# Two gated feed-forwards by seven block products for eight, with modulation loads moved to an earlier stage

## The chip, the cores and the metric

The kernel runs on one core of a Trainium2 chip. TensorE (PE) multiplies, VectorE (DVE), ScalarE (ACT) and GpSimd (POOL) do elementwise work, and SyncE (SP) issues most transfers. The metric is the device time of one execution in microseconds (us), lower is better, as the median of several runs.

## The reference, cut to what matters

A residual stream h of 512 tokens x 1024 features, batch 1, goes through two blocks, all in float32. The first block has sliding-window attention, a feed-forward with a causal convolution, a gated delta net, and the second such feed-forward. The second block, to which the change belongs, is modulated: nine vectors of 1024 numbers come from the condition c.

```python
def modulate(h, shift, scale):
    return h * (1 + scale[:, None, :]) + shift[:, None, :]

def swiglu(h, w_in, w_down):
    g, u = jnp.split(h @ w_in, 2, axis=-1)      # w_in 1024 x 5632
    return (jax.nn.silu(g) * u) @ w_down        # w_down 2816 x 1024
...
mod = jax.nn.silu(c) @ w_ada[l] + b_ada[l]
sh1, sc1, gt1, sh2, sc2, gt2, sh3, sc3, gt3 = jnp.split(mod, N_ADA, axis=-1)

h = modulate(rmsnorm(x, g_ffn1[l]), sh1, sc1)
x = x + 0.5 * gt1[:, None, :] * swiglu(h, w_ffn1_in[l], w_ffn1_down[l])
...
x = x + gt2[:, None, :] * (y @ w_out[l])

h = modulate(rmsnorm(x, g_ffn2[l]), sh3, sc3)
x = x + 0.5 * gt3[:, None, :] * swiglu(h, w_ffn2_in[l], w_ffn2_down[l])
```

## The kernel before, in words

**Layout.** Features lie on the 128 partitions and tokens along the free dimension, so h is eight tiles of 128 x 512. Each product of matrices in float32 is three passes of TensorE in the fp32r type: a weight tile w is split into a rounded high part wh and the rest wl, the moving operand x into xh and xl, and `mm3` adds wh·xh, wh·xl and wl·xh into one PSUM tile of 128 x 512.

**Weights.** The host packs all weights into blocks of 512 KB in the order in which the program takes them: 8 tiles of 128 x 128, 128 x 1024 numbers. `wtile` loads a block into a raw tile `wr` on SP's queue, ScalarE casts it to `wh` (CAST), VectorE subtracts for `wl`. In the delta-net stage alone (`by_dma`), `wl` is made in another way: ScalarE writes -wh and a transfer that GpSimd issues adds the raw block to it from memory. The raw, high and low tiles share twelve wide buffers of 128 x 1024 (pool "b"), with at most 3 raw, 4 high, and 4 low at a time (WRAW, WPART).

**Stages.** They run in the order swa, ffn0, gdn, ffn1, glu1, mix, glu2, final. ffn0 and ffn1 are the convolution feed-forwards of the first block, glu1 and glu2 the gated ones of the second. In `glu_ffn`, m runs over 22 pairs of tiles, gate m and up 22 + m. A tile is `gemm`: 8 k, 24 matmuls on 512 columns. ScalarE takes silu of the gate, VectorE multiplies by up, and `split` gives xh and xl for the down projection. That runs in two parts, after m = 10 and after m = 21 (`to_residual`): eight output tiles of 11 k each, added to h with the gate vector. The last two output tiles of a stage are computed in halves of 256 tokens, and the next stage's norm (`norm_halves`) and first three tiles (`gemm_halves`) too, so that a stage's first matmuls stand beside the norm of the second half.

**Modulation.** 72 blocks of w_ada (`ada`) are loaded into `wa` and reduced by one VectorE instruction each, against silu(c). 24 are done in ffn0, one for each m; 48 in glu1, three for each m below 16.

**Order.** A recorder collects all operations in program order. A planner gives each a cost and a priority, which is the program order plus a bias, and writes one static order for each engine; line L406, in the recorder, issues them all, so rows are told apart by tile names. PSUM has eight banks with caps by use (BANKS: three for `mm`). `nc.after` gives operations a further predecessor.

Of the kernel before, what the change touches and what calls it, by code (L numbers as in the profile page):

```python
# [19 lines left out]
KD = D // 128  # L20
# [474 lines left out]
class Kernel:  # L495
# [48 lines left out]
    def ps(self, shape=(128, S), tag="ps", bufs=None):  # L544
        return self.nc.pool_tile(self.pp, list(shape), F32, "ps", self.nm(tag), 8, BANKS[tag])

# [754 lines left out]
    def norm_modulated(self, n):  # L1301
# [9 lines left out]
                nc.vector.scalar_tensor_tensor(l, u, shift[:, k:k + 1], h.bitcast(F32), ALU.add, ALU.subtract)  # L1311
        return xs

    def gated(self, gate):
        def add(m, ps, t):
            self.nc.vector.scalar_tensor_tensor(self.h[m][:, t], ps, gate[:, m:m + 1], self.h[m][:, t],
                                                ALU.mult, ALU.add)
        return add
# [11 lines left out]
            nc.scalar.copy(t[r0 + 32:r0 + 64], sin[r0 + 32:r0 + 64])  # L1330
            self.tab.append(t)

    def glu_ffn(self, i, fill=lambda m: None):
        nc = self.nc
        xs = self.norm_modulated(f"ffn{i}")
        hs = []
        head = self.gemm_halves([(f"glu{i}", 0), (f"glu{i}", 22), (f"glu{i}", 1)], xs)
        tile = lambda m: head.pop(0) if head else self.gemm(f"glu{i}", m, xs)
        for m in range(22):
            if i == 1 and m == 16:  # L1340
                nc.after = (len(nc.ops) - 1,)
                self.tables()
                nc.after = ()
            g = self.act(name="g")
            nc.scalar.activation(g, tile(m), AF.Silu)
            nc.vector.tensor_tensor(g, tile(22 + m), g, ALU.mult)
            hs.append(self.split(g))
            fill(m)
            if m % 11 == 10:
                self.to_residual(f"glu_down{i}", hs, m - 10, self.gated(self.gain[f"ffn{i}"][2]), 2 if m == 21 else 0)  # L1350
                hs = []

# [253 lines left out]
    def run(self, out, stages):  # L1606
        nc = self.nc
        self.load()
        self.nsink = self.cp.tile([128, 16], F32, name="nsink")
        nc.vector.tensor_scalar_mul(self.nsink, self.v("sinks", 0, 16), -1.0)  # L1610
        self.ident16 = self.cp.tile([128, 128], BF16, name="ident16")
        nc.vector.tensor_copy(self.ident16, self.c("ident"))
        self.chunk16 = self.cp.tile([128, 128], BF16, name="chunk16")
        nc.vector.tensor_copy(self.chunk16, self.c("chunk")[:, 384:])
        second = any(s in stages for s in ("glu1", "mix", "glu2"))
        ada, bias = [], []
        if second:
            ada, bias = list(range(72)), list(range(32))
        for s in stages:
            if s != "swa" and ada and not hasattr(self, "cs"):  # L1620
                self.ada_start()
            self.by_dma = s == "gdn"
            if s == "swa":
                self.attention()
            elif s in ("ffn0", "ffn1"):
                if s == "ffn1" and bias:
                    self.bias_start()
                def fill(m, i=int(s[-1])):
                    nc.after = (len(nc.ops) - 1,)
                    for _ in range(min(1, len(ada)) if i == 0 else 0):  # L1630
                        self.ada(ada.pop(0))
                    for _ in range(min(2, len(bias)) if i == 1 else 0):
                        self.bias(bias.pop(0))
                    nc.after = ()
                self.conv_ffn(int(s[-1]), fill)
            elif s == "gdn":
                self.gdn()
            elif s in ("glu1", "mix", "glu2"):
                while len(ada) > 48:
                    self.ada(ada.pop(0))  # L1640
                if len(bias) == 32:
                    self.bias_start()
                while bias:
                    self.bias(bias.pop(0))
                for i in {"glu1": (0,), "mix": (1, 2), "glu2": ()}[s]:
                    self.ada_end(i)
                if s == "mix":
                    self.mixer()
                else:
                    def fill(m):  # L1650
                        nc.after = (len(nc.ops) - 1,)
                        for _ in range(min(3, len(ada))):
                            self.ada(ada.pop(0))
                        nc.after = ()
                    self.glu_ffn(int(s[-1]), fill)
# [48 lines left out]

WRAW, WPART = 3, 4


# [9 lines left out]
```

## Time and profile before

| what | value |
|---|---|
| median of 3 runs | 2667.7 us (2664.78 to 2669.11) |
| the profiled execution's own time | 2670.8 us |
| its span, first to last instruction | 2668.7 us |
| TensorE busy, share of the span | 2617.2 us, 98% |
| VectorE busy | 1660.8 us, 62% |
| ScalarE busy | 1197.7 us, 45% |
| GpSimd busy | 146.9 us, 6% |
| mean granted clock of TensorE | 0.993 of full |
| transfers of weights on SP's queue (q1) | 271.39 MB, 31.4% of 16 DMA engines |

A busy engine in such a page is one with an instruction under way. Matmuls overlap, so the length that a row gives for a matmul (0.28 us on 256 columns) is longer than the distance from one start to the next, which is what a stream of them costs.

### The profile page before, as it was taken

Reading aid. Unit: us, or ns where it says so; the run is one execution under the profiler, and the core shown is the slowest. Engines: PE = TensorE matmul, PEld = TensorE weight load, DVE = VectorE, ACT = ScalarE, POOL = GpSimd, SP = SyncE. Lnnn points to the kernel's source line nnn. Section 1 sums busy time; section 2 is a strip of 40 time slices with the busy share of each in tenths; the row PEclk is TensorE's granted clock in tenths of the full one; section 3 lists DMA queues with packets and bytes.
Section 4 is the critical chain, followed back from the end, with each engine's and each line's share of the span. In section 5 each row is a group of like instructions: output and inputs, shape, how many; then the busy total and the mean of one; then the engine's idle time right before and its main releaser. Section 6 shows DMA issues by size and latency. Waiting matters only on the chain.

```text
span 2668.7 us, 36809 instructions
## 1 busy us (share of the span) xinstructions
PE 2617.2 (98%) x14108; PEld 2146.1 (80%) x14108; DVE 1660.8 (62%) x3559; ACT 1197.7 (45%) x2258; POOL 146.9 (6%) x238
## 2 busy tenths in 40 slices
PE   7999999999999999999999999999999999999998
PEld 6678888887878787877878888888877778988887
DVE  8977535548796878785354376464679656633334
ACT  5754323338777776643233232133454444332221
POOL 3410000001111111000000000000000000000000
PEclk9999999999999999999999999999999999999999
DMA  4123434445473746433333357463221233233231
GB/s 153 41 64 127 148 107 132 143 140 134 110 162 96 158 103 156 101 101 111 101 119 95 95 169 245 139 214 104 88 80 56 86 109 101 88 96 101 95 95 63
DMA packets 93359, 308.33 MB, mean 116 GB/s; under 512 B 10368, under 2 KB 18816, under 8 KB 93184
## 3 DMA queue, kind: packets, MB, share of 16 engines
q1 hardware_dynamic: 83680, 271.39, 31.4%
q0 software_dynamic: 9360, 34.08, 7.5%
q8 instruction: 110, 1.80, 0.3%
q14 instruction: 65, 0.53, 0.1%
q10 hardware_dynamic: 144, 0.52, 0.1%
HBM read 298.61 MB, written 7.34 MB: 115 GB/s over the span
## 4 chain that ended last, share of the span: by engine, by line
PE 59%; DVE 2%; ACT 1%; issue 0%; DVEq 0%
PE mm L406 54%; PE ps L406 5%; DVE wl L406 0%; DVE u L406 0%; DVE xl L406 0%; DVE fin L406 0%; PE mx L406 0%; ACT kmla L406 0%; DVE n_2t L406 0%; DVE sq L406 0%; DVE top L406 0%; ACT xts L406 0%; DVE kmla L406 0%; DVE xt L406 0%; DVE n_2y L406 0%
## 5 line engine op out<-in xcount | busy, mean ns | idle before, releaser
L406 PE MATMUL mm<-xh,wh 128*128 128x512 f32 (+1 forms) x3444 | 1317.7, 384 | 9.7 <-ACT xh L406 9.7
L406 PE MATMUL mm<-xl,wh 128*128 128x512 f32 (+1 forms) x3444 | 1320.5, 384 | 1.4 <-DVE xl L406 1.3
L406 PE MATMUL mm<-xh,wl 128*128 128x512 f32 (+1 forms) x3444 | 1318.7, 383 | 3.0 <-DVE wl L406 2.0
L406 PEld LDWEIGHTS mm<-xh,wh 128*128 128x128 f32 x3444 | 647.6, 188 | 132.1 <-ACT xh L406 10.4
L406 PEld LDWEIGHTS mm<-xh,wl 128*128 128x128 f32 x3444 | 647.7, 188 | 130.2 <-issue 6.5
L406 PEld LDWEIGHTS mm<-xl,wh 128*128 128x128 f32 x3444 | 648.1, 188 | 128.9 <-issue 7.3
L406 ACT CAST wh<-wr 128x1024 fp32r<-128x1024 f32 (+1 forms) x415 | 434.2, 1048 | 582.8 <-PE mm L406 404.8
L406 DVE TENSOR_TENSOR wl<-wr,wh 128x1024 fp32r<-128x1024 f32 (+1 forms) x350 | 428.0, 1223 | 313.1 <-ACT wh L406 173.9
L406 DVE CUSTOM_DVE_ANT_0 wa<-wa,cs,vec 128x1024 f32<-128x1024 f32 x72 | 92.4, 1283 | 53.8 <-DMA wa<-in_w_dram 53.7
L406 DVE SCALAR_TENSOR_TENSOR y<-mm,vec,y 128x511 f32<-128x511 f32 x80 | 59.8, 747 | 73.0 <-ACT y L406 71.6
L406 DVE TENSOR_TENSOR xt<-xt,mm 128x512 f32<-128x512 f32 (+1 forms) x72 | 48.1, 671 | 89.0 <-PE mm L406 88.7
L406 POOL DMA_DIRECT2D wl<-in_w_dram x65 | 56.3, 866 | 829.8 <-DMA wr<-in_w_dram 421.1
L406 DVE TENSOR_TENSOR g<-mm,g 128x512 f32<-128x512 f32 x44 | 30.3, 689 | 109.3 <-PE mm L406 108.6
L406 ACT ACTIVATE sq<-xt 128x512 f32<-128x512 f32 (+1 forms) x69 | 38.7, 570 | 124.5 <-DVE xt L406 124.5
L406 DVE SCALAR_TENSOR_TENSOR xt<-mm,mod,xt 128x512 f32<-128x512 f32 (+1 forms) x47 | 31.5, 671 | 92.5 <-PE mm L406 92.2
L406 ACT ACTIVATE wl<-wh 128x1024 fp32r<-128x1024 f32 x65 | 68.7, 1059 | 39.4 <-PE mm L406 34.7
L406 ACT CAST xh<-g 128x512 fp32r<-128x512 f32 x44 | 27.3, 621 | 130.3 <-DVE g L406 130.3
L406 DVE SCALAR_TENSOR_TENSOR y<-g,gcw,y 128x511 f32<-128x511 f32 (+2 forms) x96 | 70.7, 746 | 6.9 <-ACT y L406 6.4
L406 ACT ACTIVATE y<-y 128x512 f32<-128x512 f32 x48 | 30.2, 632 | 80.7 <-DVE y L406 80.6
L406 DVE TENSOR_TENSOR y<-mm,y 128x512 f32<-128x512 f32 x48 | 32.9, 687 | 45.6 <-PE mm L406 45.6
L406 DVE TENSOR_TENSOR sq<-sq,sq 128x512 f32<-128x512 f32 (+1 forms) x68 | 43.6, 642 | 15.7 <-ACT sq L406 15.5
L406 ACT ACTIVATE g<-mm 128x512 f32<-128x512 f32 x44 | 26.2, 595 | 58.2 <-PE mm L406 58.2
(323 smaller groups left out, 2578.5 us busy)
## 6 DMA issues: line engine op xcount, KB each, us to landing
wr<-in_w_dram SPq DMA_DIRECT2D x413, 512.0 KB, 3.5
wa<-in_w_dram SPq DMA_DIRECT2D x72, 512.0 KB, 3.9
wl<-in_w_dram POOLq DMA_DIRECT2D x65, 512.0 KB, 6.7
xt<-in_xt_dram SPq DMA_DIRECT2D x8, 256.0 KB, 6.3
bias<-bo SPq DMA_DIRECT2D x8, 256.0 KB, 4.1
bi<-bias SPq DMA_DIRECT2D x8, 256.0 KB, 4.4
out_dram<-fin SPq DMA_DIRECT2D x8, 256.0 KB, 2.3
bias<-bo SPq DMA_DIRECT2D x8, 192.0 KB, 1.9
```

Of the source, the lines that this page charges most:

```text
L406: fn(*args, **kw)
```

## The change

**Seven products.** From pair m = 3 on, gate and up tile are computed together as one product of 2 x 2 blocks. The blocks of the weights are gate or up (rows) by even or odd k (columns, four k each, 128 x 512 numbers); those of x are even or odd k by first or second 256 tokens. By Strassen and Winograd's scheme seven products of sums replace eight products. Each is 4 k x 3 passes on 256 columns, in a PSUM bank of tag `sb`.

**Parts of weights.** `seven_weights` loads two raw blocks `ww` for a pair (up to four at a time) and makes seven parts `wo` (up to WSUM = 8), each with its high and low half. All seven high halves are casts by ScalarE. The low halves of parts 1, 2 and 4, which are blocks of the weights as they are, come from ScalarE's -x and a GpSimd transfer of 256 KB that adds the raw block; parts 6, 5, 7 and 3 are sums, made on VectorE (`ws`), which subtracts for their low halves too. `nc.after` lets a raw block be loaded once the product eleven marks back has been reached.

**Sums of x and the start.** `norm_seven` keeps the halves of x apart and makes four sums for each two k, on GpSimd and VectorE, with their splits. The head has four tiles in halves, then two more (before: three in halves).

**Moved.** The 48 modulation loads go from glu1 to ffn1, three for each m from 8 on. `tables`, some tables for the mixer, goes from m = 16 to m = 21 in glu1.

```diff
-BANKS = {"mm": ("mm", 3), "ps": ("small", 6), "mx": ("mx", 2)}
+BANKS = {"mm": ("mm", 3), "ps": ("small", 6), "mx": ("mx", 2), "sb": ("sb", 8)}
...
+    def seven_weights(self, name, m0, m1, ks):
...
+        for m in (m0, m1):
+            self.blocks.append([(name, k[i], m) for i in range(2) for k in ks])
+            t, d = self.wide("ww", F32, ("ww", 4)), self.I["w"][len(self.blocks) - 1]
+            nc.after = self.marks[-11:][:1]
+            nc.sync.dma_start(out=t[:, :2 * w], in_=d[:, :2 * w])
...
+        def parts(x, again=None):
+            t = self.wide("wo", F32R, ("wo", WSUM))
+            h, l = t[:, :w], t[:, 512:512 + w]
+            nc.scalar.copy(h, x)
+            if again is None:
+                nc.vector.tensor_tensor(l, x, h.bitcast(F32), ALU.subtract)
+            else:
+                nc.scalar.activation(l, x, AF.Copy, scale=-1.0)
+                nc.gpsimd.dma_start(out=l, in_=again.bitcast(F32R), accum_op=ALU.add)
+            return h, l
...
+        out = {1: parts(a11, source[0])}
+        s1 = combined(a21, a22, ALU.add)
+        s2 = combined(s1, a11, ALU.subtract)
+        out[6] = parts(s2)
+        out[5] = parts(s1)
+        s3 = combined(a11, a21, ALU.subtract)
+        out[7] = parts(s3)
+        out[2] = parts(a12, source[1])
+        s4 = combined(a12, s2, ALU.subtract)
+        out[3] = parts(s4)
+        out[4] = parts(a22, source[3])
...
+    def seven(self, name, m0, m1, ks, xs, done):
...
+        nc.scalar.copy(p1, product(1))
+        nc.vector.tensor_tensor(u2, product(6), p1, ALU.add)
+        nc.scalar.copy(p5, product(5))
+        nc.vector.tensor_tensor(u3, product(7), u2, ALU.add)
+        nc.vector.tensor_tensor(u2, u2, p5, ALU.add)
+        nc.vector.tensor_tensor(p5, u3, p5, ALU.add)
+        done(0, first, product(2), p1)
+        done(0, second, product(3), u2)
+        done(1, second, p5, None)
+        done(1, first, product(4), u3)
...
-        head = self.gemm_halves([(f"glu{i}", 0), (f"glu{i}", 22), (f"glu{i}", 1)], xs)
+        head = self.gemm_halves([(f"glu{i}", x) for x in (0, 22, 1, 23)], xs, tag="sb")
+        self.marks = [len(nc.ops)]
+        head += self.gemm_halves([(f"glu{i}", x) for x in (2, 24)], xs, tag="sb")
+        xs = sums()
...
-                    for _ in range(min(1, len(ada)) if i == 0 else 0):
+                    for _ in range(min(1 if i == 0 else 3 * (m >= 8), len(ada))):
                         self.ada(ada.pop(0))
...
-                while len(ada) > 48:
+                while ada:
                     self.ada(ada.pop(0))
...
+WSUM = 8
```

Two places show what the planner makes of it. The first is VectorE's order at the start of glu1, around the norm of the second half: sq is the sum of squares, n128 the reciprocal root, u the scaled x, xl and xs its low halves, t123 and t343 begin the names of sums of x, and the wl are low halves of the head's blocks. Before:

```order
L406 TENSOR_TENSOR sq2929_3013<-sq2929_3013,sq2946_3030 128x256
L406 TENSOR_TENSOR wl2968_3052<-wr2966_3050,wh2967_3051 128x1024
L406 TENSOR_SCALAR n128_2e2948_3032<-ps2947_3031 128x2
...
L406 SCALAR_TENSOR_TENSOR n128_2y2949_3033<-n128_2t2950_3034,n128_2y2949_3033 128x2
L406 TENSOR_TENSOR wl2982_3066<-wr2980_3064,wh2981_3065 128x1024
L406 SCALAR_TENSOR_TENSOR u2952_3036<-xt_70,gain_ffn1_2991,ps2951_3035 128x256
...
L406 SCALAR_TENSOR_TENSOR xl2909_2993<-u2952_3036,mod_570,xh2908_2992 128x256
...
L406 SCALAR_TENSOR_TENSOR xl2923_3007<-u2959_3043,mod_570,xh2922_3006 128x256
L406 TENSOR_TENSOR wl2992_3076<-wr2990_3074,wh2991_3075 128x1024
L406 TENSOR_TENSOR g2972_3056<-mm2970_3054,g2972_3056 128x512
```

After:

```order
L406 TENSOR_TENSOR sq2978_3062<-sq2978_3062,sq2991_3075 128x256
L406 TENSOR_SCALAR n128_2e2993_3077<-ps2992_3076 128x2
...
L406 SCALAR_TENSOR_TENSOR n128_2y2994_3078<-n128_2t2995_3079,n128_2y2994_3078 128x2
L406 TENSOR_TENSOR ws3063_3147<-ww3061_3145 128x512
L406 SCALAR_TENSOR_TENSOR u2957_3041<-xt_70,gain_ffn1_3039,ps2996_3080 128x256
...
L406 SCALAR_TENSOR_TENSOR xs2997_3081<-u2957_3041,mod_570,xs2997_3081 128x256
...
L406 SCALAR_TENSOR_TENSOR xs2972_3056<-u2964_3048,mod_570,xs2971_3055 128x256
L406 SCALAR_TENSOR_TENSOR t343026_3110<-u2958_3042,step2956_3040,u2957_3041 128x256
L406 SCALAR_TENSOR_TENSOR t343026_3110<-u2958_3042,mod_570,t123025_3109 128x256
L406 TENSOR_TENSOR wl3009_3093<-wr3007_3091,wh3008_3092 128x1024
L406 TENSOR_TENSOR wl3012_3096<-wr3010_3094,wh3011_3095 128x1024
L406 TENSOR_TENSOR xl3028_3112<-t123025_3109,xh3027_3111 128x512
```

Before, the low halves of the head's third and fourth block (wl2968, wl2982) stand ahead of the second half's sixteen steps; after, those of the third and fourth (wl3009, wl3012) stand behind them and behind sums of x, and a sum of weights (ws3063) stands where wl2982 stood.

The second place is ScalarE's order in the steady part of glu1, one pair. Before, it is the two casts of blocks, the silu and the cast of the product:

```order
L406 CAST wh3033_3117<-wr3032_3116 128x1024
L406 ACTIVATE g3002_3086<-mm3003_3087 128x512
L406 CAST wh3037_3121<-wr3036_3120 128x1024
L406 CAST xh3011_3095<-g3002_3086 128x512
L406 CAST wh3047_3131<-wr3046_3130 128x1024
```

After, with what each instruction waits for in brackets (PE: the last matmul that read the buffer; DMAHW: a load; DMASW: a GpSimd transfer); wo3150 is part 4 of the pair before, and wo3169, 3170, 3172, 3173, 3175 and 3176 are parts 6, 5, 7, 2, 3 and 4 of the pair itself:

```order
L406 CAST wo3150_3234<-ww3139_3223 128x512 [waits DMAHW5_49,PE_49]
L406 ACTIVATE wo3150_3234<-ww3139_3223 128x512
...
L406 CAST wo3169_3253<-ws3168_3252 128x512 [waits DVE_49,PE_49]
L406 CAST wo3170_3254<-ws3167_3251 128x512 [waits DMASW3_49,PE_49]
...
L406 CAST wo3172_3256<-ws3171_3255 128x512 [waits PE_49]
...
L406 CAST wo3173_3257<-ww3164_3248 128x512 [waits DMASW4_49,PE_49]
L406 ACTIVATE wo3173_3257<-ww3164_3248 128x512
L406 CAST wo3175_3259<-ws3174_3258 128x512 [waits DMASW7_49,Activation_49]
L406 CAST xh3160_3244<-g3136_3220 128x512 [waits DVE_49]
L406 CAST wo3176_3260<-ww3165_3249 128x512 [waits DMAHW7_49,PE_49]
L406 ACTIVATE wo3176_3260<-ww3165_3249 128x512
```

Two instructions of 1024 columns have become seven casts and three negations of 512, some of which wait for TensorE. Part wo3173 lies in the buffer that wo3150 had; its cast waits for the product that wo3150 served.

## Rows read from the trace of the kernel before

**Rows 1.** The page, busy time of each engine (share of the span)

```profile
PE 2617.2 (98%) x14108; PEld 2146.1 (80%) x14108; DVE 1660.8 (62%) x3559; ACT 1197.7 (45%) x2258; POOL 146.9 (6%) x238
```

**Rows 2.** Chain of waits, 1580 to 1700 us: start, length, what

```profile
1579.94 120.13 PE mm L406 x530
```

**Rows 3.** Windows: length, busy us (instructions) by engine, PEclk, DMA share, GB/s

```profile
core 0: us, PE busy (x) PEld busy (x) DVE busy (x) ACT busy (x) POOL busy (x), PEclk, DMA share, GB/s
1580.00:1600.00 20.00, 20.00 (x90) 16.56 (x89) 13.14 (x18) 6.75 (x8) 0.00 (x0) 1.00 0.79 258
...
1680.00:1700.00 20.00, 20.00 (x90) 16.57 (x89) 7.30 (x9) 4.21 (x4) 0.00 (x0) 1.00 0.41 132
2340.00:2360.00 20.00, 20.00 (x90) 16.57 (x89) 7.30 (x8) 6.65 (x8) 0.00 (x0) 1.00 0.33 106
```

**Rows 4.** Timeline of TensorE, matmuls on 256 columns: start, length, what

```profile
1534.08 0.28 PE L406 MATMUL mm<-xl,wh 128*128 128x256 f32 x1
...
1534.68 0.28 PE L406 MATMUL mm<-xh,wh 128*128 128x256 f32 x1
1534.80 0.28 PE L406 MATMUL mm<-xl,wh 128*128 128x256 f32 x1
```

**Rows 5.** Chain of waits, 1530 to 1570 us, start of glu1

```profile
1538.27 8.71 PE mm L406 x72
1546.98 0.34 PE ps L406 x4
...
1550.17 0.22 PE ps L406 x2
1550.39 2.15 PE mm L406 x17
```

**Rows 6.** Timeline of VectorE at the start of glu1 and in it

```profile
1539.25 1.26 DVE L406 SCALAR_TENSOR_TENSOR u<-xt,gain_ffn,ps 128x256 f32<-128x256 f32 x3
1540.42 1.27 DVE L406 SCALAR_TENSOR_TENSOR xl<-u,mod,xh 128x256 fp32r<-128x256 f32 x3
...
1545.09 0.42 DVE L406 TENSOR_TENSOR sq<-sq,sq 128x256 f32<-128x256 f32 x1
1545.43 0.87 DVE L406 SCALAR_TENSOR_TENSOR xl<-u,mod,xh 128x256 fp32r<-128x256 f32 x2
...
1560.29 0.69 DVE L406 TENSOR_TENSOR g<-mm,g 128x512 f32<-128x512 f32 x1
1560.89 1.22 DVE L406 TENSOR_TENSOR wl<-wr,wh 128x1024 fp32r<-128x1024 f32 x1
...
1589.85 1.28 DVE L406 CUSTOM_DVE_ANT_0 wa<-wa,cs,vec 128x1024 f32<-128x1024 f32 x1
```

**Rows 7.** Timeline of ScalarE in the delta-net stage

```profile
680.24 1.06 ACT L406 ACTIVATE wl<-wh 128x1024 fp32r<-128x1024 f32 x1 [2.91 <-PE mm L406]
...
687.58 0.63 ACT L406 ACTIVATE t<-z 128x512 f32<-128x512 f32 x1
688.11 1.04 ACT L406 ACTIVATE wl<-wh 128x1024 fp32r<-128x1024 f32 x1
```

**Rows 8.** DMA queues, 575 to 1110 us: packets, MB, share of 16 engines

```profile
q0 software_dynamic: 9360, 34.08, 37.6%
q1 hardware_dynamic: 9996, 35.12, 18.8%
```

**Rows 9.** Timeline of GpSimd in the delta-net stage

```profile
681.60 0.86 POOL L406 DMA_DIRECT2D wl<-in_w_dram  x1 [4.58 <-ACT wl L406]
```

**Rows 10.** The tile wl: its GpSimd transfers (ns), and all its landings

```profile
L406 POOL DMA_DIRECT2D wl<-in_w_dram x65: 853/862/1032, 584.7 to 1103.9; - x65
...
DMA to landing us min/median/max: 5.2/6.7/8.9
```

**Rows 11.** DMA issues, 1580 to 1680 us: count, size, median us to landing

```profile
wr<-in_w_dram SPq DMA_DIRECT2D x18, 512.0 KB, 4.7
```

**Rows 12.** Windows of the second convolution feed-forward, columns as in rows 3

```profile
1180.00:1220.00 40.00, 40.00 (x233) 30.75 (x232) 23.32 (x45) 14.88 (x22) 0.00 (x0) 1.00 0.40 126
1345.00:1385.00 40.00, 40.00 (x224) 29.11 (x223) 26.28 (x44) 15.88 (x22) 0.00 (x0) 1.00 0.39 119
```

**Rows 13.** Chain of waits in the same stage, two of its periods

```profile
1189.62 10.65 PE mm L406 x46
...
1201.82 10.65 PE mm L406 x46
```

**Rows 14.** Window of the delta-net stage, columns as in rows 3

```profile
575.00:1110.00 535.00, 521.15 (x3465) 433.15 (x3463) 403.18 (x1175) 388.04 (x966) 78.27 (x107) 0.98 0.57 130
```

More of the change, by code (lines that the diff above doesn't have):

```diff
@@ L1312, in norm_modulated, with norm_seven, sums @@
         return xs
+    def norm_seven(self, n):
+        nc = self.nc
+        gain, shift, _ = self.gain[n]
+        step = self.small([128, KD // 2], "step")
+        sh = shift.rearrange("p (k two) -> p k two", two=2)
+        nc.vector.tensor_tensor(step, sh[:, :, 1], sh[:, :, 0], ALU.subtract)
+        first, second = HALVES
+        us = [self.act(name="u") for _ in range(KD)]
+        xs = [{} for _ in range(KD)]
+        pairs = [(self.act(F32R, name="xs"), self.act(F32R, name="xs")) for _ in range(KD // 2)]
+        for t, R in self.norm_halves():
+            for k in range(KD):
+                u = us[k][:, t]
+                if k % 2:
+                    h, l = (x[:, t] for x in pairs[k // 2])
+                else:
+                    x = self.act(F32R, name="xs")
+                    h, l = x[:, first], x[:, second]
+                nc.vector.scalar_tensor_tensor(u, self.h[k][:, t], gain[:, k:k + 1], R, ALU.mult, ALU.mult)
+                nc.scalar.activation(h, u, AF.Identity, bias=shift[:, k:k + 1])
+                nc.vector.scalar_tensor_tensor(l, u, shift[:, k:k + 1], h.bitcast(F32), ALU.add, ALU.subtract)
+                xs[k][t.start] = h, l
+        def sums():
+            out = []
+            for k in range(0, KD, 2):
+                (u11, u12), (u21, u22) = ((us[k + i][:, first], us[k + i][:, second]) for i in range(2))
+                t12, t34 = self.act(name="t12"), self.act(name="t34")
+                t1, t2, t3, t4 = t12[:, first], t12[:, second], t34[:, first], t34[:, second]
+                s2 = shift[:, k + 1:k + 2]
+                nc.gpsimd.tensor_tensor(t1, u12, u11, ALU.subtract)
+                nc.vector.scalar_tensor_tensor(t2, u22, s2, t1, ALU.add, ALU.subtract)
+                nc.vector.scalar_tensor_tensor(t3, u22, step[:, k // 2:k // 2 + 1], u12, ALU.add, ALU.subtract)
+                nc.vector.scalar_tensor_tensor(t4, u21, s2, t2, ALU.add, ALU.subtract)
+                x = {1: xs[k][0], 2: xs[k + 1][0], 3: xs[k + 1][first.stop]}
+                for (i, j), y in (((5, 6), t12), ((7, 4), t34)):
+                    h, l = self.split(y)
+                    x[i], x[j] = (h[:, first], l[:, first]), (h[:, second], l[:, second])
+                out.append(x)
+            return out
+        return xs, sums
     def gated(self, gate):
@@ L1331, in tables, with glu_ffn, done @@
             self.tab.append(t)
[L1333 removed]
+    def glu_ffn(self, i):
         nc = self.nc
[L1335 removed]
+        xs, sums = self.norm_seven(f"ffn{i}")
+        ks = [(k, k + 1) for k in range(0, KD, 2)]
         hs = []
[L1337 to L1338 removed]
+        head = self.gemm_halves([(f"glu{i}", x) for x in (0, 22, 1, 23)], xs, tag="sb")
+        self.marks = [len(nc.ops)]
+        head += self.gemm_halves([(f"glu{i}", x) for x in (2, 24)], xs, tag="sb")
+        xs = sums()
         for m in range(22):
[L1340 to L1343, printed above, removed]
             g = self.act(name="g")
[L1345 to L1346 removed]
+            if m < 3:
+                nc.scalar.activation(g, head[2 * m], AF.Silu)
+                nc.vector.tensor_tensor(g, head[2 * m + 1], g, ALU.mult)
+            else:
+                u = self.act(name="gu")
+                def done(j, t, ps, more):
+                    if more is not None:
+                        nc.vector.tensor_tensor((u if j else g)[:, t], ps, more, ALU.add)
+                        ps = (u if j else g)[:, t]
+                    if j == 0:
+                        nc.scalar.activation(g[:, t], ps, AF.Silu)
+                    else:
+                        nc.vector.tensor_tensor(g[:, t], g[:, t], ps, ALU.mult)
+                self.seven(f"glu{i}", m, 22 + m, ks, xs, done)
             hs.append(self.split(g))
[L1348 removed]
             if m % 11 == 10:
+                if i == 1 and m == 21:
+                    nc.after = (len(nc.ops) - 1,)
+                    self.tables()
+                    nc.after = ()
                 self.to_residual(f"glu_down{i}", hs, m - 10, self.gated(self.gain[f"ffn{i}"][2]), 2 if m == 21 else 0)
@@ L1649, in run @@
                 else:
[L1650 to L1655, printed above, removed]
+                    self.glu_ffn(int(s[-1]))
             elif s == "final":
```

31 lines of the change are left out of this document (28 added, 3 removed).

## The prediction

> **What bounds it now.** The page first: TensorE is busy 2617.2 of 2668.7 us [rows 1]. Busy time can hide short waits, so the chain of waits comes next. From 1579.94 us in the first feed-forward of the second block (glu1) it is one piece of 120.13 us with 530 matmuls and no step on another engine [rows 2]: nothing is waited for, and one matmul on 512 columns costs 120.13/530 = 0.2267 us. The windows say the same of glu2 and of the stretch of the down projection (1680 to 1700): TensorE 20.00 of 20 us, VectorE 7 to 13 us [rows 3]. So in these stages only fewer TensorE microseconds, or new waits, change the time. They differ in transfers: the DMA engines are 79% busy at 1580 us, where the modulation loads that the change moves still pass, and 33% in glu2.
>
> **Products.** A pair of gate and up tiles is 2 tiles x 8 k x 3 passes = 48 matmuls on 512 columns, 48 x 0.2267 = 10.88 us. Seven products of 4 k x 3 passes are 84 matmuls on 256 columns. Their pitch is in the timeline of the halves: six steps from 1534.08 to 1534.80, 0.120 us [rows 4]; that is 0.007 more than half of 0.2267. So 84 x 0.120 = 10.08 us, 0.80 less a pair; 19 pairs in each of two feed-forwards give 38 x 0.80 = **30.5 us less**. At 0.121, which the chain's 8.71 us for 72 such matmuls gives [rows 5], it is 27. Three more head tiles in halves cost 72 x (0.240 - 0.2267) = 0.96 us in each, **1.9 more**.
>
> The Trainium skill ("TensorE: Matmul & The Clock Gate", section "Back-to-back issue gap") gives N/2.4 + 2.5 ns for an isolated matmul on N columns, an estimate of 215.8 and 109.2 ns here, so 1.19 us a pair, 45 in all and a sum of about -26. The rows above are 11 ns longer at either width; the measurement decides, and that surplus, which doesn't shrink with the columns, is what speaks against seven narrow products.
>
> **Side work of a pair.** VectorE loses two subtractions of 1024 columns and gains four sums and four subtractions of 512, seven additions and two silu products of 256. One step of 512 takes 0.60 us (1560.29 to 1560.89), one of 256 takes 0.34 (1545.09 to 1545.43) [rows 6]. So 9 x 0.60 (eight on weights and one xl) + 9 x 0.34 = 8.5 us of 10.08. ScalarE has ten steps of 512 on weights at about 0.53 (687.58 to 688.11 [rows 7]), one xh, two copies and two silu of 256: about 7 us. By their sums neither bounds. The cover is thin on VectorE: 1.6 us in a pair. The DMA engines: in the delta-net stage (575 to 1110 us), where the same accumulate transfers ran at twice the size, q0 took 37.6% of 535 us for 65 of them, 3.1 us of all 16 engines each; q1 took 18.8% for 66 or 67 loads, 1.5 each [rows 8]. Two loads and three accumulates of half the size make 3.0 + 4.6 = 7.7 of 10.08 us, 76%: near the 79% that glu1 had without a wait.
>
> **The new wait.** Parts 1, 2 and 4 get their low half by ScalarE writing -x and a GpSimd transfer adding the raw block. There are eight part buffers and seven parts in a pair, so the part for product 2 takes the buffer of the previous pair's part for product 4 (the second order excerpt above shows it waiting for TensorE). This closes a loop: product 4 ends; cast 0.53; negation 0.63 (the duration of one on 512); 0.30 until the POOL row begins (680.24 + 1.06 to 681.60 [rows 7, 9]); the landing L; then products 2, 3 and 4, 36 x 0.120 = 4.32 us. The period is 5.78 + L, and it costs nothing while L is at most 10.08 - 5.78 = **4.3 us**; from L = 5.1 a pair takes as long as before. L of a 256 KB accumulate isn't in this trace. Of 512 KB it is 5.2, 6.7 and 8.9 us (least, median, greatest [rows 10]), under raw loads that overlap. Half the bytes are 1.55 us of engine time less: 3.7 from the least, 5.2 from the median. Upper bound: 6.7, if size didn't matter; lower bound 3.7. The loop leaves the transfer of part 2 between the raw loads, so I take the middle, 4.45, 0.15 over what is free. A second loop runs through part 4, whose raw block is released late and whose transfer meets both loads of the next pair; it allows about 5, and I add 0.05 for it. The first pairs of each stage find free buffers, which leaves 36: 36 x 0.20 = **7 more** (0 at L = 4.3 or less; 36 x 2.4 = 86 at 6.7).
>
> **Start of each stage.** Before, three head tiles' first halves cover the norm of the second half; the broadcast of that norm came inside the third (1550.17 us [rows 5]). After, the blocks of tiles 3 and 4 get their low halves on VectorE behind that norm's 16 steps and three steps of sums (the first order excerpt). 24 matmuls fewer in front are 2.9 us uncovered, less 0.5 because VectorE has a 0.60 sum where a 1.14 subtraction stood; then wl3009 comes after 19 x 0.39 + 1.14 = 8.6 us (a STT of 256: 1.17/3 between the rows at 1539.25 and 1540.42 [rows 6]), when TensorE, with 5.8 us of second halves, has some two thirds of the third tile left to do without it: 1 us. The other nine sums of x and eight xl, 9 x 0.39 + 8 x 0.60 = 8.3 us, cost nothing beside four head tiles of 48 x 0.120 = 5.8 us each. About 3.3 at each of two starts, **6.5 more**; bounds 0, if the two subtractions could run ahead of the norm after all, and 2 x 8.6 = 17, if TensorE found nothing else to do.
>
> **Down projection in the middle.** Its loads now share twelve wide buffers with raw blocks and parts of pair 11 onwards. A block lasts 24 x 0.2267 = 5.4 us; a load that must wait for a buffer takes 4.7 to land (DMA rows of glu1 [rows 11]), 0.95 to cast, 1.14 to subtract, 6.8: up to 1.4 late for each of some five blocks, while products of pair 11 fill in. I take 1.5 a stage, **3 more** (0 to 14).
>
> **Late modulation.** 48 loads and steps of 1.28 us leave glu1, where they cost TensorE nothing [rows 2], so their removal gains nothing by itself; it makes room for VectorE and the DMA engines. They go to ffn1, three for each m from 8 on. There VectorE is busy 23.3 to 26.3 of 40 us [rows 12]; an m is 1201.82 - 1189.62 = 12.2 us long [rows 13], so 7.1 to 8.0 of it; with 3 x 1.28 [rows 6] it is 10.9 to 11.8 of 12.2, and the DMA share goes from 0.40 to 0.40 + 3 x 1.5/12.2 = 0.77. It fits with little to spare: **1 more** (0, to 16 x 0.5 = 8 if VectorE ran half a microsecond over in each m).
>
> **Sum:** -30.5 + 1.9 + 7 + 6.5 + 3 + 1 = -11.1 us. Against the profiled execution's own 2670.8 that is 2659.7. The median, 2667.7, is 3.1 less than that execution, so I predict 2656.6 for the median.
>
> **Rivals.** (A) The loops never bind and the starts stay covered, since L is at its 3.7 and the pools leave slack: -30.5 + 1.9 + 4 = -24.6, 2643. For it speaks the period with L = 3.7, 9.5 us; against it that the landing's median with 1.55 off is 5.2. (B) The accumulate lands late. The turning point: the sum is zero at -1.6 (two pairs) + 12.4 (other terms) + 36 x (5.78 + L - 10.88), L = 4.8. At 5.5 it is 10.8 + 36 x 0.40 = 25 more, 2693; at 6.7, 10.8 + 36 x 1.60 = 68 more, 2736. For it: the 6.7 median, and 76% busy DMA engines with the raw loads on the other queue; against it: half the bytes, and four of the seven parts need no such transfer. (C) The waits take just the gain: L of 4.6 to 4.9 or VectorE's queue 0.3 late a pair, since it runs parts, sums and silu in one order and its spare is 1.6; within 5 us of 2668. (D) A lock between VectorE and GpSimd delays each transfer's descriptors by one VectorE step: 0.69 us [rows 6] on the loop, 36 x 0.69 = 25 more on my sum, 2681. In the delta-net stage VectorE was busy 403 of 535 us [rows 14], while the POOL rows stay at 853 to 1032 ns [rows 10]: hardly a delay there.
>
> The Trainium skill ("SBUF — State Buffer", sections "SBUF: two separate sides" and "Who interferes with whom") says that a VectorE step in a two-port mode shuts GpSimd out of a shared port pair, so that it cannot write a transfer's descriptors, and counts additions of two tensors as harmless for that; this would be (D). The trace's narrow 853 to 1032 agrees with the milder reading.
>
> **How the numbers follow.** A measurement of this kernel tells about 0.2%, 5.3 us, from no change. The forecast (2648 to 2662) 0.40, A 0.22, C 0.17, B 0.15, D 0.06. Faster is forecast plus A, with a little of C: 0.64; same 0.16; slower B, D, the rest of C: 0.20. The range, 2638 to 2684, leaves out the lowest fifth of A (0.04) and what B holds beyond L = 5.25 (0.13); the likeliest case alone holds 2648 to 2662.
>
> **What would show it.** Right: in the steady stretch of glu1 a pair's period of 10.1 to 10.4 us, matmuls on 256 columns 0.120 apart, the POOL row of part 2 about 1.44 us after product 4, landing 4 to 5 us; a TensorE gap of 3 to 4 us where the second-half norm of each glu stage starts; ffn1 unchanged within 2 us; the mid-stage down projection with gaps below 1.5 us a block. Wrong: the idle time ahead of TensorE in glu2 ends by DMA landings of wo with more than 0.5 us a pair (B), by VectorE's sums (C), or POOL rows above 1.1 us (D); ffn1 longer by over 5 us would put the fault in the moved modulation.

## The result and the profile after

The changed kernel takes 2737.7 us in the median (2730.2 to 2740.6, 4 runs) beside 2668.4 of the kernel before on the same chip: a ratio of 1.0257, 95% interval 1.0244 to 1.0270. I had forecast 2656.6, so the sign was wrong. The profiled span is 2738.8 us, 70.1 longer than before.

The page, busy time and the chain that ended last by line; the first line answers to [rows 1]:

```profile
PE 2625.8 (96%) x15616; PEld 2220.6 (81%) x15620; DVE 1882.4 (69%) x4133; ACT 1372.4 (50%) x2692; POOL 252.2 (9%) x360
PE mm L406 35%; PE sb L406 10%; DMA wo<-in_w_dram 6%; PE ps L406 5%; DMA ww<-in_w_dram 0%; DVE fin L406 0%; DVE u L406 0%; PE mx L406 0%; ACT kmla L406 0%; DVE wl L406 0%; DVE n_2t L406 0%; ACT wo L406 0%; DVE xl L406 0%; DMA wr<-in_w_dram 0%; DVE top L406 0%
```

The second line before the change, where no transfer stands in it:

```profile
PE mm L406 54%; PE ps L406 5%; DVE wl L406 0%; DVE u L406 0%; DVE xl L406 0%; DVE fin L406 0%; PE mx L406 0%; ACT kmla L406 0%; DVE n_2t L406 0%; DVE sq L406 0%; DVE top L406 0%; ACT xts L406 0%; DVE kmla L406 0%; DVE xt L406 0%; DVE n_2y L406 0%
```

TensorE isn't less busy, although it has 30 us less to do, and a transfer of parts (wo) stands in the chain that ended last. Windows of 20 us in glu1 and glu2, columns as in [rows 3]:

```profile
1580.00:1600.00 20.00, 16.90 (x141) 16.69 (x141) 11.65 (x22) 12.27 (x26) 3.77 (x5) 1.00 0.54 127
1600.00:1620.00 20.00, 15.28 (x126) 14.88 (x125) 14.32 (x30) 11.34 (x24) 4.00 (x5) 1.00 0.77 175
2380.00:2400.00 20.00, 17.58 (x134) 17.18 (x133) 13.70 (x28) 11.71 (x24) 4.30 (x5) 0.91 0.58 126
```

TensorE, 20.00 of 20 before, is now idle for 2.4 to 4.7 of 20, and VectorE isn't at its limit either (12 to 14). The chain of waits in glu1 (start, length, what; sb is a product, wo a part, ww a raw block, POOLq GpSimd's queue, and issue is time in which nothing that the profile shows is waited for):

```profile
1599.68 7.33 DMA wo<-in_w_dram
1607.02 0.04 issue
1607.06 1.47 PE sb L406 x10
1608.53 0.03 POOLq L406
1608.56 1.43 issue
1609.99 0.02 POOLq L406
1610.01 0.24 POOL wo L406
1610.24 1.97 issue
1612.22 0.01 POOLq L406
1612.23 7.59 DMA wo<-in_w_dram
1619.82 0.04 issue
1619.86 11.83 PE sb L406 x84
```

It is one loop for a pair: a part lands at 1607.02, product 4 runs to its end (1.47 us), that frees the buffer for the next pair's part 2 (cast and negation, to 1610.00), ScalarE takes part 4 behind it, whose transfer starts at 1612.23 and lands 7.59 us later. The period is 1.47 + 1.48 + 2.23 + 7.59 = 12.8 us for 10.08 of work. After the second landing the next 84 matmuls run without a wait; more on that below. The waits of TensorE for landings of parts from glu1 on (in total, times, longest):

```profile
PE sb L406 <- DMA wo<-in_w_dram: 54.6, 26, 3.7
```

In the steady pairs 21 idle times stand ahead of the third matmul of product 4, for part 4's landing, 54.0 us in all; three of 0.5 to 1.0 us stand ahead of product 2. GpSimd's three transfers in that time and SP's two raw loads:

```profile
1610.00 0.86 POOL L406 DMA_DIRECT2D wo<-in_w_dram  x1 [8.27 <-DVE g L406]
1612.23 0.86 POOL L406 DMA_DIRECT2D wo<-in_w_dram  x1 [1.36 <-ACT wo L406]
1613.68 0.86 POOL L406 DMA_DIRECT2D wo<-in_w_dram  x1 [0.59 <-ACT sc L406]
```

```profile
1612.31 0.33 SPq L406 DMA_DIRECT2D ww<-in_w_dram  x1
...
1612.87 0.33 SPq L406 DMA_DIRECT2D ww<-in_w_dram  x1
```

The first transfer (part 2, 1610.00) lands in 3.9 us. The second (part 4) sets off with both raw loads of a later pair, and 1.4 us ahead of the next pair's part 1; it takes 7.6, and part 1 takes 7.9. The raw loads come just then because the mark that releases them is the start of product 7 of the pair that TensorE is in. Other pairs show how much hangs on this moment: where the first raw load starts 0.6 or 0.7 us behind part 4's transfer (1625.98, 1837.33, 2427.02, 2451.62, 2584.81), that lands in 5.7 to 5.8 us, and where it starts 0.8 or 0.9 behind (1665.52, 1812.06), in 4.3 and 4.0; where both start with it or ahead of it, 6.5 to 8.8. What the idle time does to the clock, in windows of 1 us around two of the waits (the last three columns: granted clock, DMA share, GB/s):

```profile
1606.00:1607.00 1.00, 0.00 (x0) 0.00 (x0) 0.29 (x1) 0.00 (x0) 0.00 (x0) 1.00 1.13 234
...
1608.00:1609.00 1.00, 1.00 (x11) 1.00 (x10) 0.44 (x2) 0.45 (x1) 0.00 (x0) 1.00 0.03 6
...
1616.00:1617.00 1.00, 1.00 (x11) 1.00 (x10) 1.00 (x3) 0.80 (x2) 0.00 (x0) 1.00 1.13 248
...
1618.00:1619.00 1.00, 0.00 (x0) 0.00 (x0) 0.87 (x2) 0.13 (x1) 0.00 (x0) 1.00 1.12 305
...
1620.00:1621.00 1.00, 1.00 (x6) 1.00 (x6) 0.00 (x0) 0.00 (x0) 0.00 (x0) 0.50 0.20 29
1621.00:1622.00 1.00, 1.00 (x6) 1.00 (x6) 0.00 (x0) 0.00 (x0) 0.00 (x0) 0.50 0.01 2
1622.00:1623.00 1.00, 1.00 (x7) 1.00 (x6) 0.70 (x2) 0.70 (x2) 0.00 (x0) 0.50 0.00 0
1623.00:1624.00 1.00, 1.00 (x9) 1.00 (x9) 1.00 (x3) 0.97 (x2) 0.25 (x1) 0.79 0.00 0
```

After the 2.5 us without work up to 1619.86 TensorE is granted 0.50, which is 1.2 of 2.4 GHz, for some 3.4 us: a matmul each 0.214 us, not 0.120. After those up to 1607.06, about as long, it stays at 1.00. Of the 19 idle times of 2.0 to 3.9 us in the steady pairs 11 go with such a stretch, of 3.4 or 6.8 us, and eight don't; one stretch more goes with two idle times of 1.1 and 1.7 us, one soon after the other. The seven pairs above whose raw loads start 0.6 us or more behind part 4's transfer each begin within such a stretch, and none of them waits at product 4: the 84 matmuls from 1619.86 take 11.83 us, 1.75 more than at full clock, and part 4 lands in time. So slow time stands partly in the place of idle time; what would be lost without it no run shows. The DMA engines are full up to 1620 and empty after 1621: all transfers of a pair are bunched into one stretch of it.

**Where 70 us went.** From the starts of neighbouring matmuls, what is over 0.2267 or 0.120 us was added up, counted as idle above 0.35 us and as slow below. In the steady pairs (ahead of each down projection, in both stages) idle time is 16.9 + 13.6 + 15.5 + 14.9 = 60.8 us in 28 pieces and slow time 28.1; before, both were 0. The starts lose 5.6 and 6.4 us, before 1.3 and 2.1. Stage lengths, from one stage's last addition to the residual to the next one's (us; ffn1 from its first convolution step):

| kernel | ffn1 | glu1 | mix | glu2 |
|---|---|---|---|---|
| before | 363.1 | 362.6 | 388.5 | 363.2 |
| changed | 364.0 | 396.9 | 388.0 | 399.8 |

-30.5 + 1.9 (products) + 60.8 + 28.1 + 8.6 (starts) + 1.5 (down projections) + 0.9 (ffn1) - 1.9 (all else) = 69.4 of 70.1.

### The profile page after: what moved, and what is told of

Read it like the earlier page. It is cut to its first block, busy times and chain, and to the rows that moved or that the text cites. A ratio compares the mean times of both kernels' runs of the same rounds, so it can differ in the third digit from the quotient of the medians.

```text
span 2738.8 us, 41406 instructions
## 1 busy us (share of the span) xinstructions
PE 2625.8 (96%) x15616; PEld 2220.6 (81%) x15620; DVE 1882.4 (69%) x4133; ACT 1372.4 (50%) x2692; POOL 252.2 (9%) x360
## 4 chain that ended last, share of the span: by engine, by line
PE 51%; DMA 7%; issue 3%; DVE 2%; ACT 1%; POOL 0%; POOLq 0%; DVEq 0%; ACTq 0%
PE mm L406 35%; PE sb L406 10%; DMA wo<-in_w_dram 6%; PE ps L406 5%; DMA ww<-in_w_dram 0%; DVE fin L406 0%; DVE u L406 0%; PE mx L406 0%; ACT kmla L406 0%; DVE wl L406 0%; DVE n_2t L406 0%; ACT wo L406 0%; DVE xl L406 0%; DMA wr<-in_w_dram 0%; DVE top L406 0%
## 5 line engine op out<-in xcount | busy, mean ns | idle before, releaser
L406 PE MATMUL mm<-xh,wh 128*128 128x512 f32 (+1 forms) x2692 | 1038.0, 386 | 8.7 <-ACT xh L406 8.7
L406 PE MATMUL mm<-xl,wh 128*128 128x512 f32 (+1 forms) x2692 | 1038.8, 386 | 1.5 <-DVE xl L406 1.5
L406 PE MATMUL mm<-xh,wl 128*128 128x512 f32 (+1 forms) x2692 | 1036.5, 386 | 3.0 <-DVE wl L406 2.0
L406 PEld LDWEIGHTS mm<-xh,wl 128*128 128x128 f32 x2692 | 506.8, 188 | 103.9 <-issue 5.9
L406 PEld LDWEIGHTS mm<-xl,wh 128*128 128x128 f32 x2692 | 507.1, 188 | 102.4 <-issue 6.8
L406 PE MATMUL sb<-xh,wo 128*128 128x256 f32 x1216 | 254.6, 299 | 53.7 <-DMA wo<-in_w_dram 51.5
L406 PEld LDWEIGHTS sb<-xh,wo 128*128 128x128 f32 x1216 | 209.6, 206 | 60.1 <-DMA wo<-in_w_dram 57.3
L406 PE MATMUL sb<-xs,wo 128*128 128x256 f32 x1368 | 187.4, 286 | 3.1 <-DMA wo<-in_w_dram 3.0
L406 PEld LDWEIGHTS sb<-xs,wo 128*128 128x128 f32 x1368 | 176.5, 195 | 5.3 <-DMA wo<-in_w_dram 4.3
L406 PE MATMUL sb<-xl,wo 128*128 128x256 f32 x608 | 179.5, 295 | 0.0
L406 DVE TENSOR_TENSOR wo<-ws,wo 128x512 fp32r<-128x512 f32 x152 | 104.2, 687 | 18.7 <-ACT wo L406 17.9
```

What stands on the lines that cost most here:

```text
L406: fn(*args, **kw)
```

## Experiments

The theories after this reading: (1) the burst: part 4 lands late because its transfer shares the DMA engines with the two raw loads and the next part 1; (2) the accumulate transfers hold each other up on GpSimd's own queue. Each run was timed beside the kernel before on its chip; ratios are to it. Unless it is said that the order stands, the planner made a new one for each edit.

**Raw loads later.**

```diff
-            nc.after = self.marks[-11:][:1]
+            nc.after = self.marks[-8:][:1]
```

> Edit: the raw blocks of a pair may be loaded three products (36 matmuls each, about 4.3 us) later than in the changed kernel; nothing else. Theory 1 (burst): the part for product 4 lands late, 7.3 to 8.2 us, because its transfer starts together with the two raw loads of a later pair and the part for the next product 1, while the part for product 2, alone on the DMA engines, lands in 3.9. With the raw loads later it should land in 4 to 5, the idle time of 2 to 3 us a pair should go, with it the stretches of lower clock behind it, and the time should be 2650 to 2680. Theory 2 (own queue): the three accumulate transfers within 3.7 us hold each other up on GpSimd's queue, raw loads or not: landing stays at 7 or more and the time at 2735 to 2742.

2796.5 us, 1.0481 (1.0463 to 1.0499). Neither theory had this. The order shows why it tells nothing of them: with later loads the planner mixed down projections into the pairs (products of pairs and of the down projection take turns from 1630 us on) and moved over 2700 lines on TensorE. Waits of TensorE for landings of parts from glu1 on add up to 72.2 us (54.6 in the changed kernel). A test that keeps the order was needed; it follows below.

**Part 4 by VectorE.**

```diff
-        out[4] = parts(a22, source[3])
+        out[4] = parts(a22)
```

> Edit: the low half of the part for product 4 comes from a VectorE subtraction instead of the negation and the GpSimd transfer; parts 1 and 2 keep theirs. Theory 1 (burst): the stall in front of the third matmul of product 4 goes, the part for product 1 still meets the raw loads and becomes the next to land last, with about 1 us idle a pair: 2665 to 2695. Theory 2 (own queue): two transfers a pair instead of three land in 4 to 5 us, no stall: 2645 to 2660. If the time stays above 2730, the transfer of part 4 was not the cause.

2676.4, 1.0029 (1.0013 to 1.0045). 61 us are back with one transfer of three; waits for landings fall from 54.6 to 6.9 us. The value lies in the burst's range.

**All parts by VectorE.**

```diff
-        out = {1: parts(a11, source[0])}
+        out = {1: parts(a11)}
...
-        out[2] = parts(a12, source[1])
+        out[2] = parts(a12)
...
-        out[4] = parts(a22, source[3])
+        out[4] = parts(a22)
```

> Edit: all seven low halves come from VectorE, no accumulate transfer and no negation is left. Both theories: no landing of a part ends an idle time of TensorE; VectorE has 8.5 + 3 x 0.60 = 10.3 us a pair against 10.08 of TensorE, so it bounds by a little: 0.2 to 0.8 us a pair, 2650 to 2680. If the time stays above 2730, sums and buffers, not landings, hold TensorE.

2668.0, 1.0002 (0.9990 to 1.0014). No wait for a landing is left. glu1 is 355.9 us long, 6.7 shorter than before, but glu2 370.5, 7.3 longer: there 11.5 us are idle in pieces around the first down projection, for ScalarE's and VectorE's steps in a planned order that mixes products as in the first run. In the steady pairs without idle time (1580 to 1660, 2500 to 2580) VectorE is busy 18.7 to 20.0 of 20 us and TensorE 20.00: at 10.3 us by my count VectorE just keeps up.

**Late modulation alone.** The kernel before with

```diff
-                    for _ in range(min(1, len(ada)) if i == 0 else 0):
+                    for _ in range(min(1 if i == 0 else 3 * (m >= 8), len(ada))):
...
-                while len(ada) > 48:
+                while ada:
```

> Edit: the kernel before with only the late modulation: the 48 loads and steps go from glu1 to ffn1, three for each m from 8 on; products stay eight. My prediction has 1 us more (0 to 8); rival: they squeeze VectorE in ffn1, 5 us more or above. Within 2664 to 2672 bears the first out.

2671.9, 1.0015 (1.0004 to 1.0026): 3.9 us more. ffn1 is 367.2 us long (363.1), glu1 and glu2 362.6 and 363.2 as before, so taking the loads out of glu1 gains nothing, as forecast. The profile has one wait each for ScalarE's xh (1.3 us) and a bias step (1.1).

**Half of each raw block, order kept.**

```diff
-            nc.sync.dma_start(out=t[:, :2 * w], in_=d[:, :2 * w])
+            def load(out, in_):
+                nc.sync.real.dma_start(out=out[:, :w], in_=in_[:, :w])
+                nc.gpsimd.real.memset(out[:, w:], 0.0)
+
+            nc.record("SP", "dma_start", load, (), dict(out=t[:, :2 * w], in_=d[:, :2 * w]))
```

> Edit: the changed kernel with the same order on TensorE, VectorE and ScalarE; of each raw block of a pair only the first half of the columns is loaded (256 KB), and GpSimd zeroes the other half, so the second half of those weights is left out of the result. The first run of this study moved the raw loads and the planner answered with another order everywhere, so it didn't test the burst; here the order stands. Theory 1 (burst with the raw loads): the transfer of part 4 starts with two raw loads of 3.0 us of all DMA engines; half of them is 1.5 us less, its landing falls from 7.3 to 8.2 to about 6, idle time per pair from 2.4 to about 1, the time to 2670 to 2700. Theory 2 (the accumulates hold each other up): landing stays at 7 or more, 2730 to 2742.

2691.9, 1.0085 (1.0069 to 1.0102), in the burst's range and 38 below the lower end of the other's. The chain of waits, one pair (L605 is the added memset):

```profile
1612.09 6.33 DMA wo<-in_w_dram
1618.42 0.04 issue
1618.46 1.47 PE sb L406 x10
1619.93 0.03 POOLq L406
1619.96 1.47 issue
1621.43 0.02 POOLq L406
1621.45 0.19 POOL wo L406
1621.64 2.02 issue
1623.66 0.01 POOLq L605
1623.67 6.20 DMA wo<-in_w_dram
```

The loop is the same, and only the landing is shorter, 6.2 for 7.6: 1.4 us, for the 1.5 of DMA work that was taken away. The period is 5.2 + 6.3 = 11.5 us; 28 of the 29 idle times in the steady pairs are 0.4 to 1.8 us long, and the granted clock stays at 1.00 behind each of them. The other one, 2.6 us up to 1595.2, is followed by 3.4 us at 0.50.

**Accumulates of 32 KB, order kept.**

```diff
-                nc.gpsimd.dma_start(out=l, in_=again.bitcast(F32R), accum_op=ALU.add)
+                def add(out, in_):
+                    nc.gpsimd.real.dma_start(out=out[:, :64], in_=in_[:, :64], accum_op=ALU.add)
+
+                nc.record("POOL", "dma_start", add, (), dict(out=l, in_=again.bitcast(F32R)))
```

> Edit: the changed kernel with the same order everywhere; each accumulate transfer adds only the first 64 of 512 columns (32 KB for 256), so most of the low halves of parts 1, 2 and 4 is left wrong. Theory 1 (burst): 1.4 us less of own work and of the two other parts'; the raw loads still run in the way, so part 4 lands in 4.5 to 6, idle 0 to 0.8 us a pair, 2648 to 2675. Theory 2 (accumulates hold each other up): landing falls to about 3 even beside the raw loads, no idle time, 2645 to 2655. A third possibility, a fixed cost of an accumulate whatever its size, would leave landing at 7 and the time above 2730.

2660.9, 0.9965 (0.9951 to 0.9980). Waits for landings fall to 1.2 us in all; the chain in glu1 is TensorE alone:

```profile
1604.93 25.00 PE sb L406 x207
```

Alone, part 2's transfer of 32 KB lands in 2.3 to 2.7 us; part 4's, beside the raw loads, still in 4.5 to 5.1 in most pairs (3.8 to 5.6 in all). So beside the raw loads even so small a transfer takes some 2 us more, as theory 1 says, and theory 2's 3 us isn't met. The allowed landing of about 5 is met, and the loop no longer bounds. The time still isn't the 2643 of my rival A: ffn1 is 4.1 us longer than before (0.9 in the changed kernel with the same order; why, no run shows), and the starts lose 4.3 us more each; -28.6 + 4.1 + 8.6 = -15.9, and the profiled span, 2655.0, is 13.7 shorter.

**Parts 1 and 4 by VectorE; parts 1 and 2 by VectorE.** The edits are lines of the third run's.

> Edit: parts 1 and 4 get their low halves from VectorE, part 2 keeps its GpSimd transfer, which in the changed kernel lands in 3.9 us; planned anew. Theory 1 (burst): no late landing is left, VectorE has 8.5 + 1.2 = 9.7 us a pair against 10.08, so no idle time in the steady pairs; with the start of each stage 5 us longer than before and ffn1 2 to 4 longer, 2650 to 2662. If part 2's transfer becomes late in its turn (6 us and more), 2670 to 2700.

2669.2, 1.0003 (0.9993 to 1.0012), slower than I gave it. Waits for landings of part 2, 10.6 us in ten pieces, are left: in the new order its transfer runs beside the raw loads now and then and lands in 3.9 to 6.1 us.

> Edit: parts 1 and 2 get their low halves from VectorE, part 4 alone keeps its GpSimd transfer; planned anew. Theory 1 (burst with the raw loads): part 4's transfer still starts with the raw loads, lands in 5.5 to 7, and idles TensorE by 0.5 to 1.5 us a pair: 2670 to 2705, clearly above the run that keeps part 2's. Theory 2 (accumulates hold each other up): alone it lands in 4, no idle time: the same time as the run that keeps part 2's, 2650 to 2662.

2685.3, 1.0053 (1.0038 to 1.0068). Part 4's transfer is now the only one on GpSimd's queue. From glu1 on it lands in 3.9 to 4.1 us where no load of 512 KB starts within 4 us of it, in 5.2 to 6.0 where one starts within 0.3 us, and in 6.0 to 7.9 where two start within 1.1 us (least, median, greatest of all 38):

```profile
DMA to landing us min/median/max: 3.9/5.4/7.9
```

With one accumulate in a pair, no other can hold it up, and it is late all the same: theory 2 is out as the cause. What the other two add in the changed kernel, where it takes 6.5 to 8.8, isn't told apart. In this order waits for landings are 12.4 us; steps of ScalarE and VectorE make more.

**A later mark for the first raw blocks.** All parts by VectorE, and

```diff
-        self.marks = [len(nc.ops)]
+        self.marks = [len(nc.ops) - 1]
```

> Edit: all low halves from VectorE, as in the third run, and the first raw blocks of each stage wait for the last matmul of the first four head tiles, one operation earlier in the recorder's list than the mark used so far; planned anew. In the planned order the low halves of the head's third and fourth block then stand ahead of the norm of the second half again. Theory: the 5.6 us that the start of a stage lost against full pace (1.3 before the change) come from these blocks, which the early raw blocks kept out of the wide buffers; with them ahead the loss falls to 1 to 3 us, two stages give 5 to 9 us less than the third run, 2659 to 2664. Rival: the shorter cover is TensorE's own, 48 matmuls instead of 72 in front of the norm; then the start stays as long, 2666 to 2670.

2645.4, 0.9924 (0.9906 to 0.9942): 21 us faster than the kernel before, and better than I expected. glu1 is 350.8 us, glu2 352.4. VectorE at the start of glu1, in the changed kernel and here:

```profile
1549.04 0.69 DVE L406 TENSOR_TENSOR ws<-ww 128x512 f32<-128x512 f32 x1
1549.71 1.26 DVE L406 SCALAR_TENSOR_TENSOR u<-xt,gain_ffn,ps 128x256 f32<-128x256 f32 x3
...
1558.40 2.36 DVE L406 TENSOR_TENSOR wl<-wr,wh 128x1024 fp32r<-128x1024 f32 x2
```

```profile
1550.15 1.22 DVE L406 TENSOR_TENSOR wl<-wr,wh 128x1024 fp32r<-128x1024 f32 x1
...
1553.32 1.22 DVE L406 TENSOR_TENSOR wl<-wr,wh 128x1024 fp32r<-128x1024 f32 x1
1554.46 1.26 DVE L406 SCALAR_TENSOR_TENSOR u<-xt,gain_ffn,ps 128x256 f32<-128x256 f32 x3
```

The two low halves stand ahead of the norm again, and the starts lose 1.8 and 2.1 us for 6.0 and 6.4 in the third run: 8.5 us of the 22.6 between the two. In every run with the early mark the starts lose 5 to 6.5 us, in the four with the later one some 2 or less, whatever the order besides. So the early raw blocks had put the low halves of the head's third and fourth block behind the norm; that it was by the wide buffers is not shown. The rival, that six tiles in halves cover less, is out. Another 12 or so are the idle stretch in glu2, which this order doesn't have. In the pairs TensorE is the chain and VectorE is full (chain of waits and windows):

```profile
1599.90 50.15 PE sb L406 x417
```

```profile
1600.00:1620.00 20.00, 20.00 (x169) 20.00 (x168) 20.00 (x43) 12.46 (x24) 0.00 (x0) 1.00 0.32 105
1620.00:1640.00 20.00, 20.00 (x168) 20.00 (x167) 20.00 (x42) 12.09 (x24) 0.00 (x0) 1.00 0.26 82
```

**Two modulation loads for each m.** In the three following, besides,

```diff
-                    for _ in range(min(1 if i == 0 else 3 * (m >= 8), len(ada))):
+                    for _ in range(min(1 if i == 0 else 2, len(ada))):
```

> Edit: as the run before in this list, and the 48 modulation loads lie in the second convolution stage at two for each of its 24 m, not three for each of the last 16. Theory: the longer convolution stage (363.1 us before, 365.5 to 367.2 with three for each) comes from VectorE being asked for 3.8 us more in 12.2; at 2.6 us it is 1 to 3 us shorter, 2656 to 2663. Rival: the first eight m carry the bias steps too, so it gets no shorter: the same as the run before, within 2 us, or longer.

2657.9, 0.9969 (0.9959 to 0.9980): 12 us worse than with three for each m from 8 on. glu1 and glu2 are the same to 0.1 us. The waits of TensorE at the start of ffn1 (in total, times, longest):

```profile
PE ps L406 <- DVE st L406: 6.3, 1, 6.3
```

The loads of the first m come where VectorE makes the bias steps (st) that TensorE waits for. VectorE is full there, and with the wait the clock falls (windows, columns as before):

```profile
1150.00:1170.00 20.00, 19.06 (x110) 14.54 (x110) 19.70 (x38) 9.88 (x17) 0.00 (x0) 1.00 0.60 187
1172.00:1182.00 10.00, 5.34 (x32) 3.81 (x32) 10.00 (x22) 2.25 (x5) 0.00 (x0) 0.52 0.34 115
```

It stands at 0.50 for 10.2 us, some 7 of them with work, which costs 3 to 4; with the 6.3 that is most of the 12. The rival in that expectation was right, and the late start of the loads in the changed kernel is worth these 12 us.

> Edit: parts 1 and 4 from VectorE, part 2 by its transfer, with the later first raw blocks and two modulation loads for each m. The seventh run of this study had idle times of 0.5 to 1.7 us in single pairs for part 2's landing at 5 us and more, about 10 us in all; the later raw blocks take 5 to 9 us off the starts. Expected 2656 to 2664; if VectorE's load was what the third run paid for in the second stage, this one is the fastest.

2680.4, 1.0052 (1.0035 to 1.0069), above the range. The same 6.3 us in ffn1, and 17.4 us of waits for landings of part 2 in glu1 and glu2.

> Edit: parts 2 and 4 from VectorE, part 1 by its transfer, with the later first raw blocks and two modulation loads for each m. Burst theory: part 1's transfer starts with the raw loads and lands in 5 to 7 us, but it is needed last, at the start of the next pair, about 7 us later: idle 0 to 0.5 us a pair, 2650 to 2665. If part 1 turns into what ends last, 2670 and above.

2673.6, 1.0022 (1.0011 to 1.0034), above the range: part 1's landing costs only 0.7 us, as I had thought, but 6.6 us in ffn1 and steps of ScalarE and VectorE in glu2 (5.8) are left.

## Why the prediction was wrong, by its own steps

- **What bounds it:** right. With the waits out of the way TensorE is the whole chain again, at 0.120 us a matmul (50.15 us for 417 in the ninth run).
- **Products, 30.5 less:** right. A pair's period in the sixth run, part 2's transfer to part 2's transfer, is 10.2 us.
- **The new wait, 7 more:** the step that failed. My first loop, through part 2, was sized well: L is 3.8 to 4.4 in most pairs, mostly below its 4.3, and TensorE waited for part 2 in three pairs alone, 1.0 us at most. The second, through part 4, "allows about 5, and I add 0.05 for it". The allowance is right: 1.47 + 1.48 + 2.23 = 5.2, so 4.9. The landing isn't: 6.5 to 8.8 us where both raw loads start with it or ahead of it, which I had taken as little over 5 although the same sentence says that this transfer meets both loads of the next pair. The DMA share of 76% that I worked out was an average; in the pair the transfers come in one burst of about 9 us and a pause. The fifth and sixth run show it with the order kept: 1.5 us less of raw loads, 1.4 us less landing; small accumulates, mostly 4.5 to 5.1. The eighth shows it with no other accumulate in the pair: up to 7.9 beside two loads, 3.9 to 4.1 without. Not tested is the other half of the loop, the eight part buffers that tie the next pair's part 2 to the end of product 4.
- **The price of a stall:** put at nothing. 11 of the 19 idle times of 2.0 to 3.9 us go with 3.4 or 6.8 us at half the clock, 28.1 us of slow time in all beside 60.8 of idle time. At the 28 idle times of 0.4 to 1.8 us in the fifth run there is no such drop. Together these two are 89 us where I had 7, part of the second in the place of the first.
- **Rival B** has 2736 for L = 6.7, next to the measured 2738. Its sign was met, idle time ahead of TensorE in glu2 that ends by landings of wo, and so was what I said for it, the raw loads on the other queue. That the number fits is chance: it is worked out for part 2's loop with no clock in it.
- **Start, 6.5 more:** 8.6, near enough (its own terms, 2.9 - 0.5 + 1, make 6.8), and the place was right, behind the norm. That the raw blocks' early start was the cause I had not seen: the ninth run.
- **Down projection, 3 more:** 1.5 at most; there is no idle time in it (65.00 of 65 us busy from 1700). **Late modulation, 1 more:** 0.9 in the changed kernel's profile, 3.9 alone in the fourth run's median, in my bounds.
- **Rival D**, a lock between VectorE and GpSimd: its mark, POOL rows above 1.1 us, doesn't appear; they stay at 853 to 1032 ns.

The Trainium skill ("DMA: Bandwidth & Descriptors", section "Queues, rings and completion order") says that each DMA engine takes turns between the queues it has work for, packet by packet. The trace agrees in so far as the accumulate on GpSimd's queue and the raw loads on SP's, started together, finish late together (7.6, and 5.0 and 8.1 us); single packets are not read here.

## What to carry to other kernels

A share of DMA time over a period says little about a transfer that a loop waits for: look which transfers the same event releases, and add up those that start with it. A stall on TensorE can cost more than its length: here idle times of 2.0 to 3.9 us went with stretches at half the clock in 11 of 19 cases, and 28 shorter ones in the fifth run with none. Where a planner makes the order, an edit that moves a load may be answered by another order everywhere; to test a cause, keep the order and change the size.

## What the runs showed of the hardware that I had not expected

- An accumulate of 256 KB alone lands in 3.9 us, one of 32 KB in 2.3 to 2.7; with 1 MB of raw loads beside it the first takes 5.7 to 8.8 and the second still 3.8 to 5.6.
- After TensorE idled 2.5 us up to 1619.86 its granted clock was 0.50 for some 3.4 us, and after 2.5 us up to 1607.06 it stayed at 1.00; after the fifth run's idle times of 0.4 to 1.8 us it was 1.00 throughout.
- VectorE steps of 256 columns with both tensors in SBUF lengthen while GpSimd subtracts two tensors in SBUF: three of them (xs) take 1.75 us in the changed kernel, and 1.27 [rows 6] otherwise. Of the changed kernel's 32 xs steps four of the six that overlap such a GpSimd instruction take 0.83 to 0.96 us, and all others 0.47 or 0.48; steps u with one tensor in PSUM stay at 0.47 beside it. The timelines of GpSimd and of VectorE at the start of glu1:

```profile
1550.34 1.62 POOL L406 TENSOR_TENSOR t<-u 128x256 f32<-128x256 f32 x2 [446.92 <-DVE u L406]
```

```profile
1550.89 1.75 DVE L406 SCALAR_TENSOR_TENSOR xs<-u,mod,xs 128x256 fp32r<-128x256 f32 x3
```

The Trainium skill ("SBUF — State Buffer", section "Who interferes with whom") states this case, two SBUF inputs against a reading GpSimd instruction, and the trace agrees.
